# The low part of every fourth weight chunk: an accumulating DMA in place of VectorE's subtraction

## The chip, the cores and the metric

The kernel runs on one core of a Trainium2 chip. The time is the device time of one execution in microseconds (us), as the median of several runs. A core has TensorE (PE: matmuls, with its weight loads shown apart as PEld), VectorE (DVE), ScalarE (ACT), GpSimd (POOL) and SyncE (SP); each works through a queue of its own in order, and they wait for one another by semaphores. Data comes from HBM through 16 DMA engines that all queues share; here SP issues the weights' loads, and POOL a few small loads.

## What is computed

A trunk of two layers on 256 tokens of 2048 features, and a last norm. In float32, cut to what matters:

```python
for layer in range(2):
    h = rms_norm(x, mix_norm[layer])
    if layer == 0:
        x = x + mixer_ab(h, ab_w_in, ab_rel_bias, ab_conv_w, ab_w_out)   # band attention, short convolution
    else:
        x = x + mixer_c(h, c_w_in, c_ln_g, c_ln_b, c_w_s, c_b_s, c_w_out)  # spatial gating
    h = rms_norm(x, ffn_norm[layer])
    x = x + (silu(h @ w_gate) * (h @ w_up)) @ w_down                      # 5632 hidden features
return rms_norm(x, final_norm)
```

Nearly all the work is matrix products of 256 tokens with float32 weights that are read once, 397 MB of them.

## The kernel before, in words

**Products.** A float32 product is taken in three passes. Each operand is split into a high part `hi`, its value rounded to float32r (a format that TensorE multiplies at its full rate), and a low part `lo`, the rest; `hi@hi + hi@lo + lo@hi` is summed in PSUM. The activations are the stationary operand, the weights stream past as the moving one.

**Chunks.** The weights are cut into 752 chunks of 256 rows by 512 columns (512 KB), in one order over the eight phases of the program: the attention layer's input and output projection (96 and 32 chunks), the feed-forward's gate and up (176) and down projection (88), then the second layer's likewise (64, 32, 176, 88). A chunk takes twelve matmuls of 128x512: two tiles of 128 rows, two halves of the tokens, three passes (lines 281 to 283 in `products`, the second of which is the first that reads `lo`).

**Preparation.** `prep(t)` makes chunk t ready. For even t it issues a load of 1 MB, two chunks, to a `raw` buffer from SP's queue. ScalarE then rounds the chunk to `whi` (line 126), and VectorE subtracts that from the raw chunk to `wlo` (line 127). There are three `raw` buffers (six chunks) and four each of `whi` and `wlo`. `prep(t + 3)` stands behind the products of chunk t, and its buffers are those of chunk t - 1; so ScalarE may start on chunk t + 3 when PE has finished chunk t - 1, and has three chunks of PE time until chunk t + 3 begins.

**Order.** Other work (transposes, norms, attention, activations) is put between the chunks at due steps. A scheduler that simulates the engines then sets the order on each engine's queue, and adds the semaphores; two neighbours in the code may change places on a queue.

**POOL's queue** has four small `pow` operations for the norms (line 201) and loads: attention's bias, the second layer's `lng`, `lnb` and `ws` (lines 576 to 579), and the last norm's gain (line 696).

Of the kernel before, what the change touches and what calls it, by code (L numbers as in the profile page):

```python
# [9 lines left out]
F32 = mybir.dt.float32  # L10
F32R = mybir.dt.float32r
AF = mybir.ActivationFunctionType
ALU = mybir.AluOpType
AX = mybir.AxisListType
PSUM = bass.MemoryType.PSUM

P = 128
S = 256
M = S // P
D = 2048  # L20
NB = 512
# [14 lines left out]
KC = 2  # L36
# [7 lines left out]
def trunk_kernel(  # L44
# [2 lines left out]
    x, mix_norm, ab_w_in, ab_rel_bias, ab_conv_w, ab_w_out, c_w_in, c_ln_g, c_ln_b,  # L47
    c_w_s, c_b_s, c_w_out, ffn_norm, ffn_w_gate, ffn_w_up, ffn_w_down, final_norm, out,
):
    """Activations are token-major in PSUM and the residual; they are the stationary  # L50
    operand, feature-major, of every projection, whose weights stream past as the moving one.

    A float32 product a @ b is taken in three float32r passes: each operand is split exactly
    into a part of twelve significant bits and the rest, and hi@hi + hi@lo + lo@hi is summed in
    PSUM (lo@lo lies below float32's last bit). The norms' per-feature gains ride on the
    transposes' evacuation, their per-token factors on the projections' evacuation.
    """
    nc = tc.nc

    const = ctx.enter_context(tc.tile_pool(name="const", bufs=1))  # L60
# [4 lines left out]
    ps_tp = ctx.enter_context(tc.tile_pool(name="ps_tp", bufs=2, space=PSUM))  # L65
    ps_ms = ctx.enter_context(tc.tile_pool(name="ps_ms", bufs=2, space=PSUM))

# [1 line left out]
    phases = []  # L69

    def phase(name, kt, blocks):
# [20 lines left out]
    chunks = []  # L92
# [5 lines left out]
    raws, parts = {}, {}  # L98
# [18 lines left out]
    def prep(t):  # L117
        if t >= len(chunks):
            return
        per = RC // KC  # L120
        if t % per == 0:
            rest = load(t)
        r = raws[t // per][:, (t % per) * KC : (t % per + 1) * KC, :]
        hi = wpool.tile([P, KC, NB], F32R, tag="whi", name="whi", bufs=W_BUFS)
        lo = wpool.tile([P, KC, NB], F32R, tag="wlo", name="wlo", bufs=W_BUFS)
        nc.scalar.copy(hi, r)  # L126
        nc.vector.tensor_tensor(out=lo, in0=r, in1=hi.bitcast(F32), op=ALU.subtract)  # L127
        parts[t] = (hi, lo)
        return rest if t == 0 else None

# [1 line left out]
    jobs, seq = [], [0]  # L132
    now = [0]

# [1 line left out]
        heapq.heappush(jobs, (now[0] + dt, seq[0], fn))  # L136
        seq[0] += 1

# [1 line left out]
    xs = [resid.tile([P, M, NB], F32, tag=f"x{n}", name=f"x{n}") for n in range(4)]  # L140
    xv = x[0].rearrange("(m p) d -> p m d", p=P)

# [35 lines left out]
    def vcol(key, i):  # L178
        return vec[:, vec_at[key] + i : vec_at[key] + i + 1]

# [1 line left out]
    class Norm:  # L182
        pass

    def new_norm(gain):
        st = Norm()
        st.gain = gain
        st.cols = None
        st.ssq = small.tile([P, M, 4], F32, tag="ssq", name="ssq")
        st.hi, st.lo = {}, {}  # L190
        return st
# [18 lines left out]
        rsqrt(st.r, ms)  # L210

    def split_to(hi, lo, src):
        """hi + lo = src, in float32r parts; src lies in PSUM."""
        nc.scalar.copy(hi, src)
        nc.vector.tensor_tensor(out=lo, in0=src, in1=hi.bitcast(F32), op=ALU.subtract)

    def transpose_pair(src, c0):
        """Two 128-column tiles of a token-major [P, M, 512] tile, each as [P, S]."""
        pt = ps_tp.tile([P, 512], F32, tag="tp", name="tp")
        for j in range(2):  # L220
            for m in range(M):
                nc.tensor.transpose(  # L222
                    out=pt[:, j * S + m * P : j * S + (m + 1) * P],
                    in_=src[:, m, c0 + j * P : c0 + (j + 1) * P],
                    identity=ident,
                )
        return pt
# [31 lines left out]
            finish_norm(st)  # L259

    class Cat:
        """The feature-major operand, in tiles of four K tiles."""

        def __init__(self, pool, tag):
            self.pool, self.tag = pool, tag
# [3 lines left out]
            self.hi[n] = self.pool.tile([P, 4, S], F32R, tag=f"{self.tag}h{n}", name=f"{self.tag}h{n}")  # L269
            self.lo[n] = self.pool.tile([P, 4, S], F32R, tag=f"{self.tag}l{n}", name=f"{self.tag}l{n}")  # L270

# [1 line left out]
    def products(ps, m, lhs, t):  # L273
        _, kt, _ = phases[chunks[t][0]]
        k0 = chunks[t][2]
# [7 lines left out]
            nc.tensor.matmul(ps[m], lhsT=b, rhs=hi[:, kk, :], start=False, stop=(k == kt - 1))  # L283

    def run(pi, lhs, evac, last=None):
        """The products of a phase; with last, the program's final chunks go by token half."""
        _, kt, blocks = phases[pi]
        ps = None
        while now[0] < len(chunks) and chunks[now[0]][0] == pi:
            t = now[0]  # L290
            _, bi, k0, _, _ = chunks[t]
            while jobs and jobs[0][0] <= t:
                heapq.heappop(jobs)[2]()
            if k0 == 0:
                ps = [ps_acc.tile([P, NB], F32, tag="acc", name="acc") for _ in range(M)]
            if last and t == len(chunks) - W_BUFS:
                for tt in range(t + AHEAD, len(chunks)):
                    prep(tt)
                with tc.manual_schedule(engines={mybir.EngineType.PE}):
                    for m in range(M):  # L300
                        for tt in range(t, len(chunks)):
                            products(ps, m, lhs, tt)
                        last(m, ps[m])
                now[0] = len(chunks)
                return
            for m in range(M):
                products(ps, m, lhs, t)
            del parts[t]
            now[0] += 1
            if k0 + KC == kt:  # L310
                evac(blocks[bi][2], ps)
            prep(t + AHEAD)

# [1 line left out]
    order = ExitStack()  # L315
    order.enter_context(
        tc.manual_schedule(engines={mybir.EngineType.Activation, mybir.EngineType.DVE})
# [5 lines left out]
    nc.vector.tensor_copy(gain0, pt[:, :KD])  # L323
    st.cols = gain0
    load_second = prep(0)
    load_x(0, 1)
    load_second()
# [12 lines left out]
    load_vectors()  # L340
    later(4, transpose_vectors)

# [1 line left out]
    mix = ExitStack()  # L344
    mpool = mix.enter_context(tc.tile_pool(name="mix_a", bufs=1))
    cat = Cat(mpool, "cat")
# [96 lines left out]
            later(6 + 2 * j, lambda j=j: attend(g, j))  # L443

    def conv_y(g):
        """The convolution's own sums, feature-major, of four tiles of features."""
        z = grp["z", g]
        ys = mpool.tile([P, 4, S], F32, tag="ys", name="ys")
        for half in range(2):
            pt = transpose_pair(z, half * 2 * P)  # L450
            zp = mpool.tile([P, 2, S + CONV - 1], F32, tag="zp", name="zp", bufs=2)
            nc.vector.memset(zp[:, :, 0 : CONV - 1], 0.0)
            nc.scalar.copy(zp[:, :, CONV - 1 :], pt.rearrange("p (a b) -> p a b", a=2))
            for j in range(2):
                kk = half * 2 + j
                f = 4 * g + kk
                y = ys[:, kk, :]
                nc.vector.tensor_scalar(
                    out=y, in0=zp[:, j, 0:S], scalar1=vcol("conv", f), scalar2=None, op0=ALU.mult
                )  # L460
                for i in range(1, CONV):
                    nc.vector.scalar_tensor_tensor(
                        out=y, in0=zp[:, j, i : i + S], scalar=vcol("conv", i * (BW // P) + f),
                        in1=y, op0=ALU.mult, op1=ALU.add,
                    )
        grp["y", g] = ys
# [93 lines left out]
        while jobs:  # L560
            heapq.heappop(jobs)[2]()

    # The pool of a mixer is given back when its last product has been issued; what is still due
    # then touches the residual alone.
    mix.close()
    st_c = new_norm("mix1")
    fst = ffn(0, 2, st_f, st_c)
    fst.close()

# [1 line left out]
    mix = ExitStack()  # L571
    mpool = mix.enter_context(tc.tile_pool(name="mix_c", bufs=1))
    us = Cat(mpool, "us")
# [57 lines left out]
            later(1 + n, block)  # L631

    def spatial(n):
        """The mixed positions of the two groups that make block n."""
        res = []
        for m in range(M):
            ps = ps_ms.tile([P, 512], F32, tag="ms", name="ms_ps")
            for j in range(2):
                g = 2 * n + j
                nc.tensor.matmul(  # L640
                    ps[:, j * GW : (j + 1) * GW], lhsT=wsT[:, g, :],
                    rhs=vt[:, m, g * GW : (g + 1) * GW], start=True, stop=True,
                )
            res.append(ps)
        gate[n] = res
# [40 lines left out]
    run(5, us, lambda n, ps: residual_evac(st_g, n, ps))  # L686
    mix.close()

# [1 line left out]
    fin = new_norm(None)  # L690
    fgs, outs = {}, {}
    part = small.tile([P, M], F32, tag="ms", name="part")
# [7 lines left out]
        fgs[n] = fg[:, :NB]  # L700

    def final_evac(n, ps):
        """What the final norm can do of a block before the last block's sums are known."""
        residual_evac(None, n, ps)
        squares(fin, n)
        gain_rows(n)
        o = resid.tile([P, M, NB], F32, tag=f"xl{n}", name=f"o{n}")
        for m in range(M):
            nc.vector.tensor_tensor(
                out=o[:, m, :], in0=xs[n][:, m, :], in1=fgs[n], op=ALU.mult  # L710
            )
        outs[n] = o
        if n == 2:
            gain_rows(3)
            nc.vector.tensor_reduce(out=part, in_=fin.ssq[:, :, 0:3], op=ALU.add, axis=AX.X)
            nc.vector.tensor_scalar(
                out=part, in0=part, scalar1=1.0 / D, scalar2=EPS, op0=ALU.mult, op1=ALU.add
            )
# [62 lines left out]
```

## Time and profile before

| | |
|---|---|
| median of the runs | 2132.92 us (2132.88 to 2132.96) |
| span of the profiled execution | 2130.4 us |
| PE busy | 2115.4 us, 99% |
| VectorE busy | 1086.5 us, 51% |
| ScalarE busy | 955.1 us, 45% |
| POOL busy | 17.8 us, 1% |
| HBM to the core | 189 GB/s on average |

The profiled execution's span, from its first instruction to its last, is 2.5 us under the runs' median, which also has what lies around the span. Busy times are sums over the span; an engine that is idle may be waiting for a buffer that another one still reads.

### The profile page before, as it was taken

The page shows a single profiled execution, that of the slowest core. Times are in us where ns is not written, and L with a number is a line of the kernel's source. Part 1 is how long each engine was busy: PE and PEld are TensorE (multiplying, and loading weights), DVE is VectorE, ACT ScalarE, POOL GpSimd, SP SyncE. Part 2 cuts the span into 40 slices and gives each one's busy share as a digit, 9 for nine tenths or more (in the row PEclk, how much of TensorE's full clock was granted, in tenths as well). Part 3 has the DMA queues.
Part 4 walks back from the last instruction along what each step waited for, and adds up shares of the span by engine and source line. Part 5 has one row for each costly group of instructions (what it writes and reads, how often), then busy time and mean ns, then how long its engine had stood idle before and what let it go on. Part 6 is the DMA issues. An engine that isn't in the chain of part 4 may idle for free.

```text
span 2130.4 us, 23444 instructions
## 1 busy us (share of the span) xinstructions
PE 2115.4 (99%) x9554; PEld 1755.9 (82%) x9554; DVE 1086.5 (51%) x1117; ACT 955.1 (45%) x1126; POOL 17.8 (1%) x37
## 2 busy tenths in 40 slices
PE   8999999999999999999999999999999999999998
PEld 7888888888888888888888888888888888888886
DVE  5545565555444554445444565555444554444443
ACT  6544445444444444444445544444444444434443
POOL 1000000000000000000000000000000000000000
PEclk9999999999999999999999999999999999999999
DMA  7555555555655555555566655555555556565553
GB/s 265 181 172 174 186 189 183 192 186 190 191 186 196 185 190 189 187 197 184 193 198 227 196 171 184 179 194 183 195 180 197 192 185 195 180 216 197 189 190 135
DMA packets 202524, 404.76 MB, mean 190 GB/s; under 512 B 6604, under 2 KB 7216, under 8 KB 202160
## 3 DMA queue, kind: packets, MB, share of 16 engines
q1 hardware_dynamic: 200480, 397.44, 56.7%
q0 software_dynamic: 1328, 4.77, 0.7%
q8 instruction: 75, 1.23, 0.2%
q10 hardware_dynamic: 608, 1.06, 0.1%
q14 instruction: 33, 0.27, 0.0%
HBM read 401.14 MB, written 2.10 MB: 189 GB/s over the span
## 4 chain that ended last, share of the span: by engine, by line
PE 99%; DMA 1%; issue 0%; SPq 0%; ACT 0%; DVE 0%; POOLq 0%; POOL 0%
PE acc L281 32%; PE acc L282 32%; PE acc L283 32%; PE tp L222 2%; DMA x<-in_x_dram 1%; PE ms_ps L640 0%; PE ms_ps L386 0%; PE ms_ps L430 0%; PE tp L418 0%; PE ms_ps L433 0%; SPq L106 0%; SPq L145 0%; ACT o L745 0%; PE tp L589 0%; ACT junk L724 0%
## 5 line engine op out<-in xcount | busy, mean ns | idle before, releaser
L127 DVE TENSOR_TENSOR wlo<-raw,whi 128x1024 fp32r<-128x1024 f32 x752 | 920.5, 1225 | 1000.8 <-ACT whi L126 1000.7
L126 ACT CAST whi<-raw 128x1024 fp32r<-128x1024 f32 x752 | 791.7, 1053 | 1106.4 <-PE acc L283 1079.5
L281 PE MATMUL acc<-whi,xh 128*128 128x512 f32 x2048 | 800.6, 392 | 0.0
L282 PE MATMUL acc<-wlo,xh 128*128 128x512 f32 x2048 | 797.7, 390 | 0.0
L283 PE MATMUL acc<-whi,xl 128*128 128x512 f32 x2048 | 797.4, 390 | 0.0
L283 PEld LDWEIGHTS acc<-whi,xl 128*128 128x128 f32 x2048 | 384.6, 188 | 80.0
L282 PEld LDWEIGHTS acc<-wlo,xh 128*128 128x128 f32 x2048 | 385.1, 188 | 78.8 <-DVE wlo L127 0.3
L281 PEld LDWEIGHTS acc<-whi,xh 128*128 128x128 f32 x2048 | 384.6, 188 | 78.5 <-ACT whi L126 0.4
L281 PE MATMUL acc<-whi,hh 128*128 128x512 f32 x704 | 274.3, 390 | 0.0
L283 PE MATMUL acc<-whi,hl 128*128 128x512 f32 x704 | 273.9, 389 | 0.0
L282 PE MATMUL acc<-wlo,hh 128*128 128x512 f32 x704 | 273.9, 389 | 0.0
L283 PEld LDWEIGHTS acc<-whi,hl 128*128 128x128 f32 x704 | 132.2, 188 | 27.5
L281 PEld LDWEIGHTS acc<-whi,hh 128*128 128x128 f32 x704 | 132.2, 188 | 27.2
L282 PEld LDWEIGHTS acc<-wlo,hh 128*128 128x128 f32 x704 | 132.2, 188 | 27.1
L281 PE MATMUL acc<-whi,cath 128*128 128x512 f32 x128 | 50.1, 392 | 0.0
L281 PE MATMUL acc<-whi,ush 128*128 128x512 f32 x128 | 50.1, 392 | 0.0
L283 PE MATMUL acc<-whi,catl 128*128 128x512 f32 x128 | 49.8, 389 | 0.0
L283 PE MATMUL acc<-whi,usl 128*128 128x512 f32 x128 | 49.8, 389 | 0.0
L282 PE MATMUL acc<-wlo,cath 128*128 128x512 f32 x128 | 49.8, 389 | 0.0
L282 PE MATMUL acc<-wlo,ush 128*128 128x512 f32 x128 | 49.8, 389 | 0.0
L541 ACT ACTIVATE sg<-acc,rstd 128x512 f32<-128x512 f32 x44 | 30.2, 690 | 19.5 <-PE acc L283 19.5
L546 DVE SCALAR_TENSOR_TENSOR hh<-acc,rstd,sg 128x512 f32<-128x512 f32 x44 | 30.9, 744 | 0.0
(116 smaller groups left out, 614.3 us busy)
## 6 DMA issues: line engine op xcount, KB each, us to landing
raw<-in_ffn_w_gate_dram SPq DMA_DIRECT2D x88, 1024.0 KB, 5.2
raw<-in_ffn_w_up_dram SPq DMA_DIRECT2D x88, 1024.0 KB, 5.2
raw<-in_ffn_w_down_dram SPq DMA_DIRECT2D x88, 1024.0 KB, 5.1
raw<-in_ab_w_in_dram SPq DMA_DIRECT2D x47, 1024.0 KB, 5.2
raw<-in_c_w_in_dram SPq DMA_DIRECT2D x32, 1024.0 KB, 5.4
raw<-in_ab_w_out_dram SPq DMA_DIRECT2D x16, 1024.0 KB, 5.0
raw<-in_c_w_out_dram SPq DMA_DIRECT2D x16, 1024.0 KB, 5.1
x<-in_x_dram SPq DMA_DIRECT2D x3, 512.0 KB, 12.2
```

What stands on the lines that cost most here:

```text
L126: nc.scalar.copy(hi, r)
L127: nc.vector.tensor_tensor(out=lo, in0=r, in1=hi.bitcast(F32), op=ALU.subtract)
L222: nc.tensor.transpose(out=pt[:, j * S + m * P : j * S + (m + 1) * P], in_=src[:, m, c0 + j * P : c0 + (j + 1) * P], identity=ident,)
L281: nc.tensor.matmul(ps[m], lhsT=a, rhs=hi[:, kk, :], start=(k == 0), stop=False)
L282: nc.tensor.matmul(ps[m], lhsT=a, rhs=lo[:, kk, :], start=False, stop=False)
L283: nc.tensor.matmul(ps[m], lhsT=b, rhs=hi[:, kk, :], start=False, stop=(k == kt - 1))
L541: nc.scalar.activation(s[:, m, :], ps[m], AF.Silu, scale=st.r[:, m : m + 1])
L546: nc.vector.scalar_tensor_tensor(out=h[:, m, :], in0=ps[m], scalar=st.r[:, m : m + 1], in1=sg[j][:, m, :], op0=ALU.mult, op1=ALU.mult,)
```

## The change

For chunks 9, 13, 17 and so on to 749 (186 of them), VectorE's subtraction is left out. ScalarE writes the negated rounding of the raw chunk into the chunk's `wlo` buffer (a second pass over the raw chunk, beside the one that makes `whi`), and a DMA from POOL's queue reads the chunk once more from HBM and adds it onto what lies there: -hi + w is the same low part. The comments that the diff also takes away are not shown; they move the lines below by some numbers (line 126 stays, the new pass is line 129, the new DMA line 130).

```diff
         nc.scalar.copy(hi, r)
-        nc.vector.tensor_tensor(out=lo, in0=r, in1=hi.bitcast(F32), op=ALU.subtract)
+        if t >= 8 and t % 4 == 1:
+            pi, bi, k0, w, c0 = chunks[t]
+            nc.scalar.activation(lo, r, AF.Copy, scale=-1.0)
+            nc.gpsimd.dma_start(
+                lo,
+                w[k0 * P : (k0 + KC) * P, c0 : c0 + NB].rearrange("(k p) n -> p k n", p=P),
+                accum_op=ALU.add,
+            )
+        else:
+            nc.vector.tensor_tensor(out=lo, in0=r, in1=hi.bitcast(F32), op=ALU.subtract)
         parts[t] = (hi, lo)
```

ScalarE's queue in the first feed-forward's gate and up projection, before. A row is a line, an operation and its operands with the buffers' numbers; `hh8` is an evacuation of transposes, the other rows are the chunks' roundings.

```order
L126 CAST whi_5629<-raw_5627 128x1024
L126 CAST whi_5647<-raw_5627 128x1024
L126 CAST whi_5665<-raw_5663 128x1024
L126 CAST whi_5697<-raw_5663 128x1024
L214 CAST hh8_5669<-tp_5671 128x512
L214 CAST hh8_5669<-tp_5678 128x512
L126 CAST whi_5715<-raw_5713 128x1024
L126 CAST whi_5731<-raw_5713 128x1024
L126 CAST whi_5749<-raw_5747 128x1024
L126 CAST whi_5765<-raw_5747 128x1024
```

The same place now.

```order
L126 CAST whi_5696<-raw_5694 128x1024
L126 CAST whi_5714<-raw_5694 128x1024
L126 CAST whi_5732<-raw_5730 128x1024
L129 ACTIVATE wlo_5765<-raw_5730 128x1024
L126 CAST whi_5764<-raw_5730 128x1024
L223 CAST hh8_5736<-tp_5738 128x512
L223 CAST hh8_5736<-tp_5745 128x512
L126 CAST whi_5783<-raw_5781 128x1024
L126 CAST whi_5799<-raw_5781 128x1024
L126 CAST whi_5817<-raw_5815 128x1024
L129 ACTIVATE wlo_5834<-raw_5815 128x1024
L126 CAST whi_5833<-raw_5815 128x1024
```

The negating pass stands ahead of the rounding of its own chunk, whose place it takes; the rounding follows it.

POOL's queue where the second layer begins, before: the loads of that layer's constants between two norms' `pow`.

```order
L201 TENSOR_TENSOR rstd_2934<-ms_2931,mhalf_90 128x2
L576 DMA lng_7842<-in_c_ln_g_dram 128x2048
L577 DMA lnb_7843<-in_c_ln_b_dram 128x2048
L579 DMA ws_7846<-in_c_w_s_dram 128x8x128
L201 TENSOR_TENSOR rstd_7830<-ms_7827,mhalf_90 128x2
```

The same place now; the second `wlo` from `c_w_in` is that of chunk 397.

```order
L130 DMA wlo_7833<-in_ffn_w_down_dram 128x2x512
L130 DMA wlo_7902<-in_c_w_in_dram 128x2x512
L585 DMA lng_7939<-in_c_ln_g_dram 128x2048
L586 DMA lnb_7940<-in_c_ln_b_dram 128x2048
L588 DMA ws_7943<-in_c_w_s_dram 128x8x128
L210 TENSOR_TENSOR rstd_7927<-ms_7924,mhalf_90 128x2
L130 DMA wlo_8017<-in_c_w_in_dram 128x2x512
```

An accumulating DMA stands directly behind these three loads.

POOL's queue at the start of the program now (before, the two last rows here were not there, and the rest read the same but for the numbers of lines and buffers); `wlo_359` is chunk 9, the first that is made this way.

```order
L368 DMA bias_177<-in_ab_rel_bias_dram 128x256 x4
L369 MEMSET bias_177 64x4x64
L210 TENSOR_TENSOR rstd_366<-ms_363,mhalf_90 128x2
L130 DMA wlo_359<-in_ab_w_in_dram 128x2x512
L130 DMA wlo_452<-in_ab_w_in_dram 128x2x512
```

The first accumulating DMA stands behind the first norm's `pow`.

## Rows read from the trace of the kernel before

**Rows 1.** The page: span, busy times, the chain that ended last by engine.

```profile
span 2130.4 us, 23444 instructions
PE 2115.4 (99%) x9554; PEld 1755.9 (82%) x9554; DVE 1086.5 (51%) x1117; ACT 955.1 (45%) x1126; POOL 17.8 (1%) x37
...
PE 99%; DMA 1%; issue 0%; SPq 0%; ACT 0%; DVE 0%; POOLq 0%; POOL 0%
```

**Rows 2.** Groups of instructions: busy, mean ns | idle before, releaser.

```profile
L127 DVE TENSOR_TENSOR wlo<-raw,whi 128x1024 fp32r<-128x1024 f32 x752 | 920.5, 1225 | 1000.8 <-ACT whi L126 1000.7
L126 ACT CAST whi<-raw 128x1024 fp32r<-128x1024 f32 x752 | 791.7, 1053 | 1106.4 <-PE acc L283 1079.5
```

**Rows 3.** Timeline, gate and up projection: start, duration, engine, instruction [idle before].

```profile
401.74 0.39 PE L282 MATMUL acc<-wlo,xh 128*128 128x512 f32 x1
401.97 0.39 PE L283 MATMUL acc<-whi,xl 128*128 128x512 f32 x1
402.20 0.19 PEld L282 LDWEIGHTS acc<-wlo,xh 128*128 128x128 f32 x1
402.39 1.05 ACT L126 CAST whi<-raw 128x1024 fp32r<-128x1024 f32 x1 [1.67 <-PE acc L283]
403.48 1.23 DVE L127 TENSOR_TENSOR wlo<-raw,whi 128x1024 fp32r<-128x1024 f32 x1 [1.49 <-ACT whi L126]
404.74 0.37 SPq L106 DMA_DIRECT2D raw<-in_ffn_w_up_dram  x1
405.11 1.05 ACT L126 CAST whi<-raw 128x1024 fp32r<-128x1024 f32 x1 [1.67 <-PE acc L283]
```

**Rows 4.** The DMA issues: count, KB each, median us from issue to landing.

```profile
raw<-in_ffn_w_up_dram SPq DMA_DIRECT2D x88, 1024.0 KB, 5.2
lng<-in_c_ln_g_dram POOLq DMA_DIRECT2D x1, 1024.0 KB, 5.4
lnb<-in_c_ln_b_dram POOLq DMA_DIRECT2D x1, 1024.0 KB, 9.0
fg<-in_final_norm_dram POOLq DMA_DIRECT2D x4, 256.0 KB, 3.5
ws<-in_c_w_s_dram POOLq DMA_DIRECT2D x1, 512.0 KB, 11.0
```

**Rows 5.** The tile `bias`: its loads of 128 KB, from issue to landing.

```profile
DMA to landing us min/median/max: 3.2/4.9/6.8
```

**Rows 6.** Stretches: us, busy (count) by engine, clock, DMA share, GB/s.

```profile
500.00:511.00 11.00, 11.00 (x51) 9.09 (x50) 4.90 (x4) 4.34 (x5) 0.00 (x0) 1.00 0.60 191
1117.00:1130.00 13.00, 13.00 (x63) 10.87 (x62) 7.73 (x12) 7.75 (x13) 2.68 (x4) 1.00 1.00 363
```

**Rows 7.** Timeline of POOL and of ScalarE where the second layer begins.

```profile
1116.93 0.58 POOL L576 DMA_DIRECT2D lng<-in_c_ln_g_dram  x1 [728.11 <-DVE x L251]
1117.50 0.55 POOL L577 DMA_DIRECT2D lnb<-in_c_ln_b_dram  x1
1118.04 0.92 POOL L579 DMA_DIRECT2D ws<-in_c_w_s_dram  x1
...
1122.10 1.05 ACT L126 CAST whi<-raw 128x1024 fp32r<-128x1024 f32 x1 [1.67 <-PE acc L283]
...
1131.15 1.05 ACT L126 CAST whi<-raw 128x1024 fp32r<-128x1024 f32 x1 [1.67 <-PE acc L283]
```

**Rows 8.** Timeline of the start: chunk 9's rounding, the first `pow`, PE's transposes.

```profile
33.66 1.03 ACT L126 CAST whi<-raw 128x1024 fp32r<-128x1024 f32 x1
...
36.38 0.73 POOL L201 TENSOR_TENSOR rstd<-ms,mhalf 128x2 f32<-128x2 f32 x1 [22.55 <-DVE ms L206]
...
37.14 1.27 ACT L367 ACTIVATE tok<-acc,rstd 128x512 f32<-128x512 f32 x2 [2.44 <-POOL rstd L201]
...
37.68 0.61 PE L281 MATMUL acc<-whi,xh 128*128 128x512 f32 x2
...
40.40 1.03 PE L222 MATMUL tp<-ident,tok 128*128 128x128 f32 x8
```

**Rows 9.** SP's own waits: queue, line, for whom, us in total, times, longest.

```profile
SPq L106 <- DVE wlo L127: 1823.6, 356, 10.3
```

## Prediction

> **What bounds the kernel now.** I read the page's busy times and the chain of waits first. PE is busy for 2115.4 of 2130.4 us, and the chain that ended last runs over PE for 99% of the span [rows 1]. All that PE leaves is 15 us, at the start and the end of the program; so work taken from another engine can give back next to nothing, and the question is only whether the change makes PE wait. The groups of instructions agree: VectorE's subtraction takes 1225 ns and had waited 1000.8 us in total for ScalarE's rounding, which takes 1053 ns and had waited 1079.5 us for PE to free its buffer [rows 2]. Both are ahead of PE.
>
> How far ahead is read from the timeline of the gate and up projection [rows 3]. A chunk's last matmul starts at 401.97, ScalarE's rounding for the chunk four later at 402.39, and the next one at 405.11: a chunk takes 2.72 us of PE. VectorE follows at 403.48, ends at 404.71, and at 404.74 SP issues the next load, since that was the second half of a raw buffer. The first reader of `wlo` in the chunk that begins here is the weight load at 402.20; in the chunk three later it is at 402.20 + 3 x 2.72 = 410.36. So a low part that is ready at 404.71 has 5.65 us to spare. The granted clock is 1.00 there, the higher of TensorE's two levels [rows 6].
>
> **The change, part by part.** It removes 186 subtractions, 186 x 1.225 = 228 us of VectorE's time. Worth on the path: nothing, since VectorE waits for ScalarE ahead of nearly every one.
>
> It adds 186 passes on ScalarE. I price one like the rounding, 1.05 us: same shape, same buffers, one operation per element [rows 2]. In four chunks, 10.88 us, ScalarE is busy for some 4.34 us without a block's evacuation [rows 6] and would be for 5.4. The pass stands ahead of its chunk's own rounding, which is thus 1.05 us later, at some 404.3 in the terms above, with 5.9 us to spare. The raw buffer is then free when the rounding ends, at 404.3 instead of 404.71, so SP's load is not later. These cost nothing as long as the spare 5.65 us stand.
>
> It adds 186 DMAs of 512 KB on POOL's queue, each behind its negating pass, and PE behind each. This is the step that decides. The pass needs the `wlo` buffer, whose last reader starts at 401.74 and takes 0.39 us [rows 3]: so it starts at 402.16 and ends at 403.21. POOL can issue at 403.24, and the data must have landed at 410.36. **The allowance is 7.1 us from issue to landing.**
>
> What POOL's DMAs take here, from issue to landing: 3.2 us for 128 KB at best [rows 5], 3.5 for 256 KB and 5.4 for 1 MB [rows 4]. These lie near one line, 2.9 us and 0.3 us per 128 KB, so a plain load of 512 KB would take 4.1 us. No row shows a DMA that adds. It must read what lies in `wlo` besides the chunk, and so handle 1 MB where a plain one handles 512 KB. My lower bound is the plain 4.1 us. The value I take is that of `lng`, 1 MB in 5.4 us, in a stretch where the DMA engines were busy all the time [rows 6], with 1.7 us to spare. The upper row is `lnb`, which landed 9.0 us after its issue behind `lng`: 2 MB in 1117.50 + 9.0 - 1116.93 = 9.6 us from the first issue [rows 7]. Between the two rows 7.1 us is reached at 1.4 MB, that is at 2.8 times the plain traffic of such a chunk. The other limit is the engines' time: the share is 0.60 with two 1 MB loads in 10.88 us [rows 6], 3.3 us a load. An adding DMA at twice a plain one's cost makes it 0.90, and 1.00 is reached at (0.40 x 10.88) / 1.63 = 2.7 times. Both say the same: up to some 2.7 plain copies it hides, above that PE waits in every fourth chunk.
>
> On that factor the Trainium skill has something, in Collectives: The Full Stack (Part 3's account of why ReduceScatter is half of AllGather): the add is done inline in the DMA engine and costs little itself, but it needs two source reads on one ring, and measured rates stood at 1.93 to 1. By that the landing here would be 1 MB's, 5.4 us, and hidden. No row of this case shows an adding DMA, so it stays open until the trace after.
>
> The Trainium skill's DMA: Bandwidth & Descriptors (Anatomy of one DMA) gives 2.0 us and bytes over 436 GB/s for a DMA from GpSimd, which for 512 KB would be an estimated 3.2 us. The rows are slower, 3.5 us for half of that [rows 4], and I keep the rows; by the page the allowance would be wider still.
>
> **Where it cannot hide.** Two places have less than the allowance. At the start the first adding DMA, of chunk 9, stands behind the first `pow` on POOL. The rounding of chunk 9 runs at 33.66 to 34.69 and the pass behind it would end at 35.8; the `pow` ends at 37.1 before, perhaps 1 to 2 us earlier now that VectorE has a subtraction less in front of it [rows 8]. Issue between 35.9 and 37.1, landing 5.4 later at 41.3 to 42.5. PE began chunk 9 at 37.68; in the new order two matmuls and the transposes of `tok` (1.03 us) stand ahead of its first `wlo`, so PE is there at 39.2 to 39.4. It waits 1.9 to 3.1 us; I take 2.5. Where the second layer begins, the DMA of chunk 397 is issued at some 1123 behind `lng`, `lnb` and `ws`, the last of which lands at 1118.04 + 11.0 = 1129.0 [rows 4, 7]. The 2.5 MB took 12.1 us, 4.8 us a MB or by the two rows above 4.2: another 1 MB lands at some 1133.2. Chunk 397 begins about 1131.0, a little before ScalarE is released at 1131.15 [rows 7]. PE waits 0 to 2 us; I take 2. The four loads of the last norm's gain, 256 KB each, put at most some 0.6 us ahead of an adding DMA, within the 1.7.
>
> **The sum** on the profiled execution: 2130.4 + 0 (VectorE) + 0 (ScalarE) + 0 (184 hidden DMAs) + 2.5 + 2 = 2134.9; with the 2.5 us that the median lies above the span, 2137. A measurement of this kernel tells some 2%, 43 us, from no change, so this is no change. Its own range is 2130 to 2160, the top for a wait of a few tenths at a tenth or two of the places.
>
> **Rivals.** *The adding DMA lands late, and PE waits in every fourth chunk.* It decides at 7.1 us from issue to landing, or a few tenths less if POOL takes up its turn slowly. Since the next such chunk takes the same buffer, no time is made up: each costs (landing - 7.1). At 8.0 us that is 186 x 0.9 = 167 us, 2304 in all; at `lnb`'s 9.0 us 186 x 1.9 = 353, 2490. At four plain copies the engines' time alone is 2 x 3.26 + 4 x 1.63 = 13.0 us in place of 10.88: 404 us, 2541. For it: no row bounds an adding DMA's cost, a load of 1 MB is issued 1 us behind it and shares the engines, and the spare is a quarter of the allowance. Against it: `lng` had the same company and took 5.4.
>
> *The loads of the raw chunks become late* because the DMA engines are fuller: SP waited 1823.6 us for buffers in 356 waits, some 5 us a load [rows 9], so a load may take 5 us more before ScalarE waits. This comes only together with the first rival, above a share of 1.00.
>
> *A gain*, if the freed VectorE let ScalarE or PE start sooner: the bound is the 15 us that PE leaves, 2118, and even that is within 2%. A gain of 2% is shut out by PE's own 2115.4 us.
>
> *The change doesn't do what it says*: the DMA could be cut into many small pieces because it adds and changes the format. Then it is many times slower than any row here, over 3000 us; what speaks against it is only that rows of 2 KB are whole on both sides.
>
> **How the numbers follow.** Hidden, 0.52; late by up to `lnb`'s 9.0 us, 0.29; later than that, or cut small, 0.17; some gain, 0.02. The time is the likeliest's, 2137. The range takes in hidden and late up to 2490, from 2128 at the bottom, and leaves out 0.19. Faster by over 2% 0.01; within 2% 0.52 and the rest of the gain, 0.53; slower 0.46.
>
> **What would show it.** In the profile after: VectorE busy near 860 us, ScalarE near 1150, 97.5 MB on the software queue, the new DMAs landing in 5 to 6.5 us, and no wait of PE for `wlo` but at chunks 9 and 397. Wrong would be: landings above 7 us at the median, with PE waiting for a DMA before line 291 some 186 times. Then the step that failed is the price of adding, taken as that of 1 MB.

## The result and the profile after

The changed kernel takes 2489.0 us (2486.6 to 2491.4) against 2132.92: 1.167 times the time before, with a 95% interval of 1.1635 to 1.1702. The forecast was 2137 with a range up to 2490. What came is the first rival, at the price that it named.

The page of the changed kernel, which answers to [rows 1 and 2]: span, busy times, the two DMA queues (packets, MB, share of the 16 engines' time), three groups.

```profile
span 2484.8 us, 23978 instructions
PE 2199.8 (89%) x9554; PEld 1762.7 (71%) x9554; DVE 864.1 (35%) x931; ACT 1128.4 (45%) x1312; POOL 242.1 (10%) x223
q1 hardware_dynamic: 200480, 397.44, 51.0%
q0 software_dynamic: 51920, 102.30, 22.2%
L136 DVE TENSOR_TENSOR wlo<-raw,whi 128x1024 fp32r<-128x1024 f32 x566 | 693.2, 1225 | 1373.3 <-ACT whi L126 1373.1
L129 ACT ACTIVATE wlo<-raw 128x1024 fp32r<-128x1024 f32 x186 | 197.2, 1060 | 608.1 <-PE acc L291 608.1
L130 POOL DMA_DIRECT2D wlo<-in_ffn_w_down_dram x44 | 53.0, 1204 | 518.8 <-ACT wlo L129 518.8
```

The busy times are where the forecast put them: VectorE 864 (some 860), ScalarE 1128 (some 1150), a negating pass 1.06 us. But PE leaves 285 us where it left 15. Who waits is read from the tile `wlo` (us in total, times) and from the landings below it.

```profile
  PEld acc L291: 346.2, 183
  PE acc L291: 269.3, 176
...
DMA to landing us min/median/max: 5.6/9.1/10.3
```

Line 291 is the matmul that reads `wlo` (line 282 before); its weight load waits 183 times and the matmul itself 176 times, for 186 new DMAs. A landing takes 9.1 us at the median where 5.4 was taken. The timeline shows one of them (start, duration, engine, instruction, idle before):

```profile
469.20 1.06 ACT L129 ACTIVATE wlo<-raw 128x1024 fp32r<-128x1024 f32 x1 [3.50 <-PE acc L291]
470.56 1.20 POOL L130 DMA_DIRECT2D wlo<-in_ffn_w_up_dram  x1 [11.72 <-ACT wlo L129]
471.22 6.35 SPq L106 DMA_DIRECT2D raw<-in_ffn_w_gate_dram  x2
...
477.39 0.61 PE L290 MATMUL acc<-whi,xh 128*128 128x512 f32 x2
479.41 0.50 PE L291 MATMUL acc<-wlo,xh 128*128 128x512 f32 x1 [1.41 <-DMA wlo<-in_ffn_w_up_dram]
...
483.14 1.20 POOL L130 DMA_DIRECT2D wlo<-in_ffn_w_gate_dram  x1 [11.38 <-ACT wlo L129]
```

The pass ends at 470.26 and POOL takes its turn 0.3 us later, which shortens the allowance of 7.1 us to 6.8. But two matmuls stand ahead of the first reader of `wlo` (the row at 477.39) where the prediction's rows had one, and that gives 0.23 us back; so some 7.1 us from issue to landing stand. This DMA took 8.8 us, 1.7 too many. The next one is issued 12.58 us later, where four chunks alone take 4 x 2.72 = 10.88, and the difference is again 1.70 us; as an estimate for all 186 that is 316 of the 354 us between the two spans.

The clock gives most of the rest. Its mean over the span is 0.986, before 0.999: 0.013 x 2484.8 = some 32 us lost in stretches at the lower of TensorE's two levels (1.2 GHz). One such stretch is shown here (us, busy and count on PE, PEld, DVE, ACT, POOL, clock, DMA share, GB/s). It follows a wait: until 152.80 PE had waited 2.43 us for a `wlo`.

```profile
152.00:153.00 1.00, 0.20 (x1) 0.20 (x2) 0.26 (x1) 0.00 (x0) 0.00 (x0) 0.87 0.92 350
153.00:156.20 3.20, 3.20 (x8) 2.53 (x9) 0.00 (x0) 0.00 (x0) 0.00 (x0) 0.51 0.50 193
156.20:158.00 1.80, 1.80 (x13) 1.58 (x13) 0.00 (x0) 1.30 (x2) 0.00 (x0) 1.00 0.00 0
```

Where the 9 us go within a DMA is seen when its time is cut in two by queue (packets, MB, share of the 16 engines). Issued at 470.56; first 470.5 to 474.5, then 474.5 to 479.

```profile
DMA packets 221, 0.45 MB, mean 113 GB/s; under 512 B 0, under 2 KB 0, under 8 KB 221
q1 hardware_dynamic: 221, 0.45, 50.5%
...
DMA packets 621, 1.21 MB, mean 268 GB/s; under 512 B 32, under 2 KB 32, under 8 KB 621
q0 software_dynamic: 272, 0.52, 63.3%
q1 hardware_dynamic: 349, 0.68, 49.5%
```

For 4 us the adding DMA (q0) moves nothing, while 221 packets of SP's next load (q1), issued 0.66 us *behind* it, run. Then the two share the engines. The next one, issued at 483.14, does the same: until 487.1 no packet of q0 and 226 of q1.

### The profile page after: what moved, and what is told of

Same layout as the page of the kernel before. It is cut to its first block, busy times and chain, and to the rows that moved or that the text cites. A ratio compares the mean times of both kernels' runs of the same rounds, so it can differ in the third digit from the quotient of the medians.

```text
span 2484.8 us, 23978 instructions
## 1 busy us (share of the span) xinstructions
PE 2199.8 (89%) x9554; PEld 1762.7 (71%) x9554; DVE 864.1 (35%) x931; ACT 1128.4 (45%) x1312; POOL 242.1 (10%) x223
## 3 DMA queue, kind: packets, MB, share of 16 engines
q10 hardware_dynamic: 608, 1.06, 0.1%
## 5 line engine op out<-in xcount | busy, mean ns | idle before, releaser
L136 DVE TENSOR_TENSOR wlo<-raw,whi 128x1024 fp32r<-128x1024 f32 x566 | 693.2, 1225 | 1373.3 <-ACT whi L126 1373.1
L291 PE MATMUL acc<-wlo,xh 128*128 128x512 f32 x2048 | 818.4, 400 | 169.3 <-DMA wlo<-in_ffn_w_up_dram 70.3
L290 PE MATMUL acc<-whi,xh 128*128 128x512 f32 x2048 | 791.7, 394 | 0.0
L129 ACT ACTIVATE wlo<-raw 128x1024 fp32r<-128x1024 f32 x186 | 197.2, 1060 | 608.1 <-PE acc L291 608.1
L291 PE MATMUL acc<-wlo,hh 128*128 128x512 f32 x704 | 285.6, 406 | 76.2 <-DMA wlo<-in_ffn_w_down_dram 76.2
L130 POOL DMA_DIRECT2D wlo<-in_ffn_w_down_dram x44 | 53.0, 1204 | 518.8 <-ACT wlo L129 518.8
L130 POOL DMA_DIRECT2D wlo<-in_ffn_w_up_dram x44 | 53.0, 1204 | 507.1 <-ACT wlo L129 507.1
L130 POOL DMA_DIRECT2D wlo<-in_ffn_w_gate_dram x44 | 53.0, 1204 | 500.4 <-ACT wlo L129 475.6
L224 DVE TENSOR_TENSOR hl<-tp,hh 128x512 fp32r<-128x512 f32 x44 | 28.3, 686 | 102.2 <-ACT hh L223 102.2
```

What stands on the lines that cost most here:

```text
L129: nc.scalar.activation(lo, r, AF.Copy, scale=-1.0)
L130: nc.gpsimd.dma_start(lo, w[k0 * P : (k0 + KC) * P, c0 : c0 + NB].rearrange("(k p) n -> p k n", p=P), accum_op=ALU.add,)
L290: nc.tensor.matmul(ps[m], lhsT=a, rhs=hi[:, kk, :], start=(k == 0), stop=False)
L291: nc.tensor.matmul(ps[m], lhsT=a, rhs=lo[:, kk, :], start=False, stop=False)
```

## The experiments

The theory at first was the one that the prediction named for this outcome: an adding DMA is slow in itself, and PE waits for it. The rivals were that a second read of the weights fills the DMA engines, that the pass on ScalarE or the lost subtraction costs something, and that format or place of the sum cut the DMA to pieces. Edits are to the changed kernel.

**e1_plain** takes the adding away and leaves DMA, pass and order. The low part of those chunks is then the raw chunk itself.

```diff
-                accum_op=ALU.add,
```

> The same DMAs without the addition: each overwrites the negated high part with the raw chunk, so the subtraction is left out of every fourth chunk's low part. If adding is what makes the DMA slow, its landing falls to 4 to 5.5 us, the issue on GpSimd from 1.20 to some 0.6 us, and the time to 2133 to 2145 us. If it is the number of rows or the change of format to float32r, the landing stays above 7.1 us and the time above 2200 us.

2137.7 us, 1.0027 (1.0016 to 1.0037). The tile `wlo`: the DMA's issues (duration in ns min, median, max; first and last start), and the landings.

```profile
L130 POOL DMA_DIRECT2D wlo<-in_ffn_w_up_dram x44: 701/713/716, 407.6 to 1870.8; - x44
...
DMA to landing us min/median/max: 4.0/4.3/9.3
```

It lands near the prediction's lower bound of 4.1 us. POOL is busy 713 ns with an issue instead of 1203. Of a DMA issued at 473.80 no packet is seen until 475.2, and from there to 477.7 its queue shows all of it:

```profile
q0 software_dynamic: 270, 0.52, 83.9%
```

The adding makes the DMA late, not the second read.

**e3_ahead** gives one chunk more of lead: a fifth pair of `whi` and `wlo`, so the allowance is 7.1 + 2.72 = 9.8 us. Room is made by a scratch tile in bfloat16 that nobody reads, and by a product formed in place.

```diff
-W_BUFS = 4
-AHEAD = 3
+W_BUFS = 5
+AHEAD = 4
...
+    prep(3)
```

> The whole change, prepared one chunk earlier (five hi and lo buffers, four chunks ahead; to make room the feed-forward's product is written in place and a scratch tile that nobody reads is bfloat16). The allowance from issue to landing grows from 7.1 to 9.8 us. If the loss is the lead alone, DMAs that land in 9.0 us plus 0.3 us on GpSimd's queue are hidden: 2135 to 2165 us. If the DMA engines or another engine's throughput bounded it, the time stays above 2400 us.

2146.4 us, 1.0066 (1.0049 to 1.0082). The tile's landings:

```profile
DMA to landing us min/median/max: 5.9/9.1/13.8
```

And a stretch of the gate and up projection:

```profile
470.00:521.00 51.00, 50.95 (x229) 41.96 (x228) 18.59 (x18) 26.11 (x28) 6.01 (x5) 1.00 0.85 236
```

The DMA takes 9.1 us as before, nearly all of it hidden (PE's weight loads still wait for a `wlo` 17 times, 10.4 us in all), at a DMA share of 0.85. So the loss is one of lead; the engines' time suffices, as the prediction had worked out (0.90 for twice a plain DMA's cost).

**e4_nodma** keeps the negating pass and leaves out the DMA, so the low parts lack the addition.

```diff
-            nc.gpsimd.dma_start(
-                lo,
...
-                accum_op=ALU.add,
-            )
```

> ScalarE's negating pass alone, the DMA and the subtraction left out (the low part of every fourth chunk is then the negated high part). If only the DMA costs, 2130 to 2137 us. If the pass on ScalarE or the new order on its queue costs something of its own, above 2150 us.

2131.45 us, 0.9994 (0.9983 to 1.0004). The pass costs nothing, and VectorE's 228 us give nothing back.

**e6_sbuf** adds from the raw buffer in SBUF in place of HBM.

```diff
+            nc.gpsimd.dma_start(lo, r, accum_op=ALU.add)
```

> The DMA adds the raw chunk from its buffer in SBUF instead of reading it from HBM again. The buffer is then held until the DMA has landed, so the 1 MB load that was issued 0.7 us behind the DMA comes after it. If sharing the DMA engines with that load costs 1.6 of the 9.0 us (16 rows an engine at 176 ns, alternating with 98 ns of the load), the landing falls to some 7.4 us and the time to 2180 to 2260 us. If the latency is fixed by the adding itself, the landing stays at 9 us and the time at some 2490 us.

2142.24 us, 1.0042 (1.0026 to 1.0058), far better than I had expected:

```profile
L130 POOL DMA_DIRECT2D wlo<-raw x186: 850/859/938, 35.3 to 2114.2; - x186
...
DMA to landing us min/median/max: 4.5/5.2/9.5
```

It adds as many bytes and lands in 5.2 us. So adding is not slow in itself, and the first theory falls as it stood. Two things differ besides the source: chunk and buffer are each contiguous there, 128 rows of 4 KB in place of 256 of 2 KB, with an issue of 0.86 us and not 1.20; and the raw buffer stays in use until the DMA has read it, so SP's next load comes later. The second gave a new theory: **order on the DMA engines**. The adding DMA takes long to its first packet, the load issued just behind it gets there first, and the DMA waits.

**e2_beside_add** takes all low parts from VectorE again and lets the DMA add onto a scratch buffer `beside` in float32, which nobody waits for.

```diff
-            nc.scalar.activation(lo, r, AF.Copy, scale=-1.0)
+            sc = wpool.tile([P, KC, NB], F32, tag="beside", name="beside", bufs=1)
+            nc.scalar.activation(sc, hi.bitcast(F32), AF.Copy, scale=-1.0)
...
-        else:
-            nc.vector.tensor_tensor(out=lo, in0=r, in1=hi.bitcast(F32), op=ALU.subtract)
+        nc.vector.tensor_tensor(out=lo, in0=r, in1=hi.bitcast(F32), op=ALU.subtract)
```

> VectorE makes every low part as before; beside it, for the same chunks, ScalarE's negated high part goes to a float32 scratch tile that nobody reads, and the DMA adds the raw chunk there from HBM (the scratch of the norms' squares is bfloat16 to make room). PE waits for none of it, and the format isn't changed on the way. If adding 512 KB from HBM costs by itself what was measured, the landing is again 8.5 to 9.2 us with 4.0 us to the first packet, and the time 2131 to 2142 us, since nobody waits. If the change of format to float32r cost it, the landing is under 6 us. If the DMA engines' fuller time were what cost, the time rises above 2180 us although nobody reads the tile.

2131.4 us, 0.9995 (0.9983 to 1.0006): all of the change's traffic, and no loss when nobody waits. The landing is 8.1 us in plain float32 too (5.8 to 9.9), so the change of format is not what makes it late. One DMA, issued at 470.35, 0.11 us behind a load; its queue share from 470.3 to 474.9 and from there to 478:

```profile
q1 hardware_dynamic: 455, 0.93, 65.4%
...
q0 software_dynamic: 269, 0.52, 92.9%
```

Nothing of the adding DMA moves until some 450 of the load's 512 rows of 2 KB have (the first few of the 455 packets are an older load's).

**e5_every8** makes every eighth chunk this way, 93 DMAs.

```diff
-        if t >= 8 and t % 4 == 1:
+        if t >= 8 and t % 8 == 1:
```

> The change for every eighth chunk only: 93 DMAs in place of 186. If each costs its own lateness of some 1.7 to 1.9 us with its clock dips, half of the loss: 2295 to 2325 us. If the loss is fuller DMA engines, much less than half: under 2230 us.

2338.13 us, 1.0965 (1.0913 to 1.1017), a little above what was expected. Landings stay at 9.1 us. Half the DMAs cost 205 us of 356: less 19 us for the clock (0.991 of a span of 2331.7), 2.0 us each, where the change by the same working has (356 - 32) / 186 = 1.7. So each pays its own lateness, and thinning them out does not lessen it; why it is a little more here was not tried.

**e7_split** cuts the DMA into two of 128 rows.

```diff
+            for k in range(KC):
+                nc.gpsimd.dma_start(
+                    lo[:, k : k + 1, :],
+                    w[(k0 + k) * P : (k0 + k + 1) * P, c0 : c0 + NB].rearrange("(k p) n -> p k n", p=P),
+                    accum_op=ALU.add,
+                )
```

> Each adding DMA cut into two of 128 rows, one for each half of the chunk, both from HBM. If the 4.0 us before the first packet are the time to make the descriptors of 256 adding rows, the first half's first packet comes some 1.3 us earlier, at 2.0 to 2.8 us, and the whole lands earlier: 2300 to 2440 us. If the 4.0 us are fixed for an add from HBM, the second half is issued later and lands later: 2480 to 2600 us.

2180.33 us, 1.0225 (1.0195 to 1.0255), much better than expected. A pair issued from 469.91 on, with the queues' packets from 471.4 to 474.2, to 475.2 and to 477.7:

```profile
q0 software_dynamic: 142, 0.26, 70.0%
...
q1 hardware_dynamic: 186, 0.38, 103.5%
q0 software_dynamic: 2, 0.00, 0.1%
...
q0 software_dynamic: 140, 0.26, 56.8%
```

The first half, issued in 0.86 us, has its first packet some 1.5 us after the issue and gets in ahead of the load; the second half finds the load there and stands still for the 1 us of the second stretch. A price per row was expected to bring the first packet at 2.0 us at the earliest, and would not make the second half stand still: that speaks for order, though this run does not shut out a price per row. The landing is 6.9 us at the median, and PE still waits for a `wlo` at 33 places, 25.5 us in all.

**e9_sbuf_rows** adds from SBUF as e6 does, but with 256 rows of 2 KB; `wlo` is padded by 16 columns so that its rows don't run together.

```diff
-        lo = wpool.tile([P, KC, NB], F32R, tag="wlo", name="wlo", bufs=W_BUFS)
+        lo = wpool.tile([P, KC, NB + 16], F32R, tag="wlo", name="wlo", bufs=W_BUFS)
+        lo = lo[:, :, 0:NB]
...
+            nc.gpsimd.dma_start(lo, r, accum_op=ALU.add)
```

> The add from the raw chunk's buffer in SBUF, with the low part's buffer padded so that its two halves don't lie end to end: 256 rows of 2 KB, as from HBM, instead of 128 of 4 KB. If the number of rows sets the time before the first packet, that goes from 1.4 back to 4.0 us, the landing to some 7.5 us, and the time to 2200 us or more. If the source (HBM or SBUF) sets it, it stays at 1.4 us, the landing at 5.2 to 5.8 us, and the time at 2140 to 2146 us.

The tile `wlo`, issues and landings:

```profile
L131 POOL DMA_DIRECT2D wlo<-raw x186: 1181/1200/1282, 35.2 to 2154.0; - x186
...
DMA to landing us min/median/max: 5.0/5.4/10.4
```

The issue takes 1.20 us as in the change, and yet it lands in 5.4 us. With the raw buffer held, next to no load is on the engines beside it, as the queues show from 471.1 to 474.1:

```profile
q0 software_dynamic: 270, 0.52, 100.2%
q1 hardware_dynamic: 25, 0.04, 3.4%
```

The rows alone are not the cause. The time, 2180.07 us, 1.0224 (1.0194 to 1.0254), is not that of waiting: PE is busy 99%, and each matmul starts a little later after the one before, 0.232 us in place of 0.227 (468.76 to 471.08 for ten; 2.72 us for a chunk's twelve in [rows 3]). PE's busy time is 2158.8 us in place of 2115.4, 43 of the 47 us. The matmuls that read `whi` are as slow as those that read `wlo`. It comes with the padded buffer, for e6 doesn't have it; why was not tried.

**e12_hold** is the run that decides. The DMA is the change's own, from HBM; one more pass over the raw chunk, to a scratch tile that nobody reads, only holds the raw buffer, and so SP's load, 1.15 us longer.

```diff
             nc.scalar.activation(lo, r, AF.Copy, scale=-1.0)
+            late = wpool.tile([P, KC, NB], mybir.dt.bfloat16, tag="late", name="late", bufs=1)
+            nc.scalar.activation(late, r, AF.Copy, scale=hi.bitcast(F32)[:, 0, 0:1])
```

> The whole change, and one pass more on ScalarE behind the chunk's rounding, which reads the raw chunk into a scratch tile that nobody reads. It holds the raw buffer 1.05 us longer, so SP issues the next 1 MB load some 1.7 us behind the adding DMA instead of 0.7. If that load overtakes the adding DMA on the engines' queues (its first packet 1.7 us after the DMA's issue, the DMA's own not ready before 1.8), the DMA now comes first: first packet at 1.8 us, landing at 5.8 to 6.8 us, and with more work on ScalarE a time of 2133 to 2165 us. If adding from HBM takes 4.0 us to start whatever else runs, the landing stays at 9.0 us and the time at 2480 us or more.

2143.64 us, 1.0053 (1.0037 to 1.0070), though it has 1.15 us more work on ScalarE for each of 186 chunks. Its timeline:

```profile
477.74 1.20 POOL L132 DMA_DIRECT2D wlo<-in_ffn_w_gate_dram  x1 [9.68 <-ACT wlo L129]
478.40 1.15 ACT L131 ACTIVATE late<-raw,whi 128x1024 bf16<-128x1024 f32 x1
479.58 0.37 SPq L106 DMA_DIRECT2D raw<-in_ffn_w_gate_dram  x1
```

The load now comes 1.84 us behind the DMA and not 0.66. The queues from 477.7 to 479.6, and from there to 483.5:

```profile
q1 hardware_dynamic: 100, 0.17, 24.8%
...
q0 software_dynamic: 272, 0.52, 92.6%
q1 hardware_dynamic: 80, 0.16, 11.1%
```

The DMA begins some 1.9 us after its issue, and now it is the load that waits. The tile's landings:

```profile
DMA to landing us min/median/max: 5.6/6.1/11.7
```

PE's waits for a `wlo` (who waited, for whom: us, times, longest):

```profile
PE acc L293 <- DMA wlo<-in_ab_w_in_dram: 5.9, 1, 5.9
PE acc L293 <- DMA wlo<-in_c_w_in_dram: 2.7, 1, 2.7
```

PE's 176 waits for a `wlo` are down to the two places that the prediction had named, at 5.9 us (2.5 forecast) and 2.7 us (2 forecast).

**e11_even** moves the change to the even chunks, whose raw buffer is still wanted for the odd chunk behind; the load that follows such a DMA is a chunk further off, and the one before it is nearer.

```diff
-        if t >= 8 and t % 4 == 1:
+        if t >= 8 and t % 4 == 0:
```

> The change for the chunks 8, 12, 16 and so on (the first half of a raw buffer) instead of 9, 13, 17: as many DMAs and passes. The load that came 0.7 us behind the DMA now comes 1.5 us ahead of it, and the next one 4 us behind. If the order against the loads decides, the DMA waits until that load is nearly through, first packet at 2.5 to 3.5 us, and then has the engines for itself: landing at 6 to 7.2 us, time 2133 to 2200 us. If the adding itself takes 9.0 us, again some 2490 us.

2168.88 us, 1.0169 (1.0154 to 1.0184), within what was expected: landing 6.5 us. The DMA issued at 479.36 meets a load that SP issued 1.8 us ahead of it, at 477.55 (first stretch, to 481.9), and then has the engines nearly alone (to 485.2):

```profile
q1 hardware_dynamic: 434, 0.88, 94.7%
q0 software_dynamic: 4, 0.01, 2.3%
...
q0 software_dynamic: 267, 0.52, 89.1%
q1 hardware_dynamic: 94, 0.17, 18.2%
```

The median of 6.5 us is so near to the allowance, and the landings scatter so far (5.7 to 11.8 us), that PE still waits for a `wlo` at 25 places, 22.1 us in all.

**e10_sbuf_late** is the best version that the runs point to: e6's DMA, without chunks 9, 13 and 397.

```diff
-        if t >= 8 and t % 4 == 1:
+        if t >= 16 and t % 4 == 1 and t != 397:
...
+            nc.gpsimd.dma_start(lo, r, accum_op=ALU.add)
```

> The add from the raw chunk's buffer, without the first two chunks and without chunk 397, the places where the prediction had a wait that cannot hide. If these places are all that is left of the loss there (2142 against 2132.8 us), 2132 to 2137 us; if not, 2140 us or more. Faster than before by more than a few us is not possible by PE's busy time.

2132.92 us, 1.0003 (0.9994 to 1.0012): the time before, with PE busy 2115.8 us of a span of 2131.0. The change can be hidden wholly; nothing beats the kernel before, since PE has nothing to give.

## Why the likeliest forecast failed and the range held

**Right: what bounds the kernel, and what the freed and added work is worth.** Zero for VectorE and zero for ScalarE are e4's 0.9994, and a gain is shut out by e10. The allowance of some 7.1 us decides as it was said to: landings of 5.2 and 6.1 us at the median hide, 6.5 in part, 9.1 do not, and with 2.72 us more 9.1 hides too.

**Right: the price of adding.** The prediction took two plain copies. In e11 a plain row costs the engines 0.947 x 16 x 2.6 / 434 = 0.091 us and an adding row 0.891 x 16 x 3.3 / 267 = 0.176 us, 1.9 times as much; in e2 the same working gives 0.106 and 0.171, 1.6 times. POOL's own queue, with as many packets in both, has 30.4% of the engines' time in e12 (adding) and 19.7% in e1 (plain), 1.5 times. Without a load in its way it lands in 5.4 to 6.1 us (e9, e12), which is `lng`'s 5.4 us and a little. The Trainium skill's rule in Collectives: The Full Stack (Part 3), that the inline add is paid by its second source read at 1.93 to 1, agrees with the highest of these ratios. By that rule alone the change would have been hidden: it prices the engines' time, which e3 shows not to be short.

**Wrong: "`lng` had the same company and took 5.4".** The size was the same, the order was not: the load behind `lng` was issued at 1119.00, 2.07 us after it. In the change SP's load is issued 0.66 us behind each adding DMA, because the rounding that ends then is the raw buffer's last reader. The prediction had noted that this load would not be later than before, and counted that as free; and where it spoke of the load behind the DMA, it reckoned with a share of the engines, not with a place in their order. A plain DMA of this shape has its first packet 1.4 us after its issue, ahead of a load that is again issued 0.66 us behind it (e1). The adding one, issued in 1.20 us, could begin at 1.9 us (e12), and by then the load is on the engines. It stands until 4 us after its issue, and shares the engines for the rest. Holding the load back by 1.2 us takes 3 us from the landing and 345 us from the program (e12), which shows the load's place behind the DMA as the cause. What the adding itself does is to begin 0.5 us later than a plain DMA and so to lose that place. So "the price of adding", which the prediction named for this outcome as the step that failed, is itself the wrong step.

**The rival's price held.** It had 186 x (9.0 - 7.1), 2490 in all, against 2489.0. It is right by a small luck: the upper row was `lnb`, a DMA behind another one, which is also what happens here, but the lateness by itself is 1.70 us in the timeline, 316 us, and the clock's 32 us, which no step had, make up the difference.

**Mis-sized: the two short places.** Forecast 2.5 and 2 us, measured 5.9 and 2.7 (e12; in the changed kernel itself the longest wait at the start is 5.1). At the start of e12 the DMA, issued at 35.67, took 9.1 us, where 5.4 was taken: three loads of 1 MB ran in the same 20 us.

**Left open.** Whether the adding DMA stands ready and is passed over, or becomes ready late because a load is running, was not tried by itself; shown is that the one whose first rows come earlier goes ahead, and that the other waits until nearly half (in the change: 221 of 512 rows) to nearly all (e2) of a 1 MB load is through. And why the clock falls after some waits and not after others was not tried.

## What to carry to other kernels

Price a DMA by what will be issued around it, within one or two microseconds before and after its own issue, and not by its bytes alone: one that is slow to start loses its place to a load issued behind it. If PE waits for it, keep the big load back until it has begun, or give the consumer a buffer more of lead. In a kernel whose PE is busy 99%, work taken from another engine buys nothing, and every new dependence on a DMA can only cost.

## What the hardware did that was not expected

- An adding DMA of 256 rows keeps POOL busy for 1.20 us with its issue, a plain one 0.71 us; with 128 rows of 4 KB the adding one takes 0.86 (e6).
- A load issued 0.66 us later overtook it, and cost it some 3 us of landing (9.1 against 6.1).
- A wait of PE of 2.4 us was followed by 3.2 us at half clock (0.51). The wait of 1.41 us that ended at 479.41 was not: from 479.40 to 483.00 the clock is 1.00. Nor was one of 2.87 us that ended at 2338.37: from 2338.30 to 2342.00 it is 1.00.
- Sixteen columns of padding in `wlo` made matmuls follow each other at 0.232 us in place of 0.227, 2% of the program.
